# A hybrid attention and MLP layer on one core: modulation in wider pieces loaded ahead, and chunked scores with stacked operands

## The chip, the core and the metric

The kernel runs on one core of one Trainium2 chip. A core has TensorE (PE, matrix multiply, with its weight loads shown as PEld), VectorE (DVE), ScalarE (ACT), GpSimd (POOL) and SyncE (SP), which here issues the DMAs. Every engine works through its own queue in order and waits on semaphores for the others. SBUF is the memory in which tiles lie, 128 partitions wide; PSUM takes the results of matmuls. The metric is the device time of one execution in microseconds; lower is better.

## The reference: what is computed

One layer over a sequence of 1024 tokens of width 1024, all float32. A conditioning vector c gives six modulation vectors; two attention head groups run side by side on one input projection; a gated MLP with a causal convolution follows.

```
mod = silu(c) @ w_ada + b_ada                 # w_ada is 1024 x 6144
sh_a, sc_a, g_a, sh_m, sc_m, g_m = split(mod, 6)

h = rmsnorm(x, g_attn_norm) * (1 + sc_a) + sh_a
q_lat, kv_lat, k_rope, ca_qkv = split(h @ w_in)
# 8 latent heads: up-projections, QK norm over 96, rotary on 32 columns, chunk-causal softmax
# 8 chunked heads: QK norm over 64, each 64-token chunk sees 9 chunks, with a relative bias
s = q @ k.T * scale + bias;  p = softmax(s);  o = p @ v
x = x + g_a * (concat(o_mla, o_ca) @ w_out)

h = rmsnorm(x, g_mlp_norm) * (1 + sc_m) + sh_m
u = causal_conv3(h @ w_up);  x = x + g_m * ((silu(gate) * val) @ w_down)
```

## The kernel before

A float32 product is made of three TensorE products: each operand is split into a rounded high part and the rest, the low part, and hi*hi, hi*lo and lo*hi are summed in PSUM. The split costs an operation on ScalarE (the high part, `hi_of`, line 75) and one on GpSimd or VectorE (the low part, `lo_of`, line 82).

**The start** (lines 194 to 259). The eight 128 x 1024 tiles of x are loaded, their squares summed on ScalarE (212), the root taken on GpSimd (115, 116), and scaled on VectorE (214). The first modulation is `silu(c) @ w_ada` for shift and scale of the mixer. It isn't a matmul: for each of eight blocks `d` of 128 columns the weights (1 MB, `adaw`, two buffers) are multiplied by c and summed on VectorE, 128 x 256 at a time, one tensor-scalar operation and seven fused ones (241, 243), and a matmul with a vector of ones sums over the partitions (246). Then block `d` of x is transposed on TensorE (221), modulated in two halves `h` of 512 tokens on ScalarE, once rounded (224) and once whole (227), and subtracted for the low part on GpSimd (`h` 0) or VectorE (`h` 1) (230): `hT[d, h]`. The first pair of chunked heads is projected as the blocks come (`qk0`, 150 to 152).

After that come the rotary tables (`rope_tables`, 262 to 326, some fifty small VectorE operations on 128 x 128 and two Sin on ScalarE), and the loads of the value weights (`f_v`, `load_w`), whose squares are summed on ScalarE (187) because a power-of-two scale for the values depends on them (`pow2_scale`, 337).

**Attention** is one list of 128 tiles of 128 query rows, first 64 of chunked, then 64 of latent heads. `Unit.scores` (633) does for one tile the score matmuls (655), on VectorE the bias and the row minimum in one operation (670; the scores are negated), on ScalarE the Exp with its row sum (681), the reciprocal (683, 684), on GpSimd the high half of the probabilities in float16 (71, tile `hl`) and on VectorE the low half (703), and then SP issues a DMA transpose of both (714, into `PT`). `Unit.values` (719) comes three tiles later and multiplies with the values (742); each group of four tiles is evicted by ScalarE and VectorE (749, 750). When a pair of heads or a half of the sequence begins, `qk_page` (611) transposes normalised queries and keys on TensorE into PSUM (615) and splits them (618 to 622). In a chunked unit the two heads of a pair lie in partitions 0 to 63 and 64 to 127 of one page, and the matmuls for a head read only its 64.

Between the tiles stand **fillers**, generators that yield after each few projection matmuls: values (`v0`), then the other query and key pairs (`qk1`, ...), the latents (`m`), the two latent up-projections (`up0`, `up1`), and the output projection of the chunked heads (`oca`). `pace` (832) runs them in proportion to the cost of the tiles. While some fillers run, `f_ada` (419) is stepped, the **second modulation**: three more 1024-wide outputs of `silu(c) @ w_ada` in twelve parts of 256 columns. For each it loads eight 128 x 256 tiles (`aw`, 128 KB, line 426) into the three buffers of tag A, which also hold the running sum `aacc` (428, 430). The gate among them is spread over the partitions by a matmul (`gate_bcast`, 451).

The order of instructions on each engine is written by a scheduler that has its own timing of every operation and follows the priorities that the program gives; `issue_after` puts a piece behind a given instruction of its engine's queue in that plan. All DMAs of this text are issued on SP's one queue, in order.

After 656 us come the output projection, the second norm, the MLP and its down projection; the change doesn't touch them.

Of the kernel before, what the change touches and what calls it, by code (L numbers as in the profile page):

```python
# [37 lines left out]
GSTEP, LAG = 2, 4  # L38
DEPTH = 3
OFF_S, OFF_P, OFF_V = 400, 200, 200  # L40
P_BUFS, HL_BUFS, PT_BUFS, TB = 3, 3, 3, 1
# [21 lines left out]
def layer_kernel(ctx, tc, I, out):  # L63
# [76 lines left out]
    def atile(name):  # L140
        return apg.tile([P, 256], F32, name=name, tag="A", bufs=3)

    def pgtile(shape, dt, name):
        return apg.tile(shape, dt, name=name, tag="pg", bufs=6)

    def gemm3(pt, pairs, start=True, stop=True):

        n = len(pairs)
        for i, (sh, sl, mh, ml) in enumerate(pairs):
            pe.matmul(pt, sh, mh, start=(start and i == 0), stop=False)  # L150
            pe.matmul(pt, sh, ml, start=False, stop=False)  # L151
            pe.matmul(pt, sl, mh, start=False, stop=(stop and i == n - 1))  # L152
# [17 lines left out]
    def load_w(name, src, ncol, he="a", ssw=None):  # L170
        tiles = []
        for k in range(ND):
# [7 lines left out]
            for c0 in range(0, ncol, 256):  # L180
# [3 lines left out]
                sp.dma_start(rw, src[:, k, c])  # L184
                if ssw is not None:
# [7 lines left out]

    xs = []
# [6 lines left out]
    wada = []  # L201

    def load_ada(d):
        w = st.tile([P, ND, 2, P], F32, name=f"adaw_{d}", tag="wa", bufs=2)
        sp.dma_start(w[:], I["w_ada_a"][d])
        wada.append(w)

    load_ada(0)
# [8 lines left out]
    def mod_transpose(src, k, h, row, pspool, psum_tag, pb, hpool, tag, tmp, nbuf, veng, leng):  # L217
# [6 lines left out]
        act.activation(pg[:, 0], pt[:], AF.Identity, scale=a, bias=b)  # L224
# [5 lines left out]
        (dve if leng == "v" else pool).tensor_tensor(pg[:, 1], v[:], f32(pg[:, 0]), op=SUB)  # L230
# [4 lines left out]
    qk0 = [ps.tile([P, 1024], F32, name=f"qk0_{i}", tag="S", bufs=2) for i in range(2)]  # L235
    for d in range(ND):
        if d + 1 < ND:
            load_ada(d + 1)
        w = wada[d]
        acc = apg.tile([P, 2, P], F32, name=f"adacc_{d}", tag="A", bufs=3)  # L240
        dve.tensor_scalar(acc[:], w[:, 0], cs[:, 0:1], None, op0=MUL)
        for k in range(1, ND):
            dve.scalar_tensor_tensor(acc[:], w[:, k], cs[:, k:k + 1], acc[:], op0=MUL, op1=ADD)  # L243
        pt = ps.tile([P, 512], F32, name=f"p_ada{d}", tag="mm", bufs=2)
        for i in range(2):
            pe.matmul(pt[:, i:i + 1], acc[:, i, :], ones[:, 0:1], start=True, stop=True)
# [15 lines left out]
    def rope_tables():  # L262
        sp.dma_start(pos_i[:], I["pos"])
        buf = [st.tile([P, 8, NT, 16], F32, name=f"rt{i}", tag="x", bufs=4) for i in range(8)]
        cnt = [0]

        def T():
            cnt[0] += 1
            return buf[(cnt[0] - 1) // 8][:, (cnt[0] - 1) % 8]

        def rnd(src, q):
            o = T()
            dve.tensor_scalar(o, src, q, MAGIC, op0=MUL, op1=ADD)
            dve.tensor_scalar(o, o, MAGIC, None, op0=SUB)
            return o

        def fma(n, c, b):
            o = T()
            dve.scalar_tensor_tensor(o, n, c, b, op0=MUL, op1=ADD)
            return o  # L280

        p1 = _grid(TWO_PI, 2.0 ** -9)
        p2 = _grid(TWO_PI - p1, 2.0 ** -21)
        p3 = TWO_PI - p1 - p2

        def reduce(src):
            n = rnd(src, 1.0 / TWO_PI)
            r = fma(n, -p1, src)
            r = fma(n, -p2, r)
            return fma(n, -p3, r)  # L290

        pf = cst.tile([P, NT], F32, name="pf")
        dve.tensor_copy(pf[:], pos_i[:])
        ang = T()
        dve.tensor_tensor(ang, pf[:].unsqueeze(2).to_broadcast([P, NT, 16]),
                          pk[:, C_INV:C_INV + 16].unsqueeze(1).to_broadcast([P, NT, 16]), op=MUL)
        nh = rnd(ang, 2.0 ** -20)
        rem = fma(nh, -(2.0 ** 20), ang)
        nm = rnd(rem, 2.0 ** -8)
        lo = fma(nm, -(2.0 ** 8), rem)  # L300
        tot = reduce(lo)
        for n, w in ((nh, 2.0 ** 20), (nm, 2.0 ** 8)):
            c = w - round(w / TWO_PI) * TWO_PI
            c1 = _grid(c, 2.0 ** -9)
            x = T()
            dve.tensor_scalar(x, n, c1, None, op0=MUL)
            x = fma(n, c - c1, reduce(x))
            y = T()
            dve.tensor_tensor(y, tot, x, op=ADD)
            tot = y  # L310
        tot = reduce(tot)
        pi_s = 3.1415925
        sn, cn, cl, c2, cl2 = T(), T(), T(), T(), T()
        dve.tensor_scalar(cl, tot, pi_s, -pi_s, op0=MIN, op1=MAX)
        act.activation(sn, cl, AF.Sin)
        dve.tensor_scalar(c2, tot, math.pi / 2, None, op0=ADD)
        dve.tensor_scalar(cl2, reduce(c2), pi_s, -pi_s, op0=MIN, op1=MAX)
        act.activation(cn, cl2, AF.Sin)

        for tab, c0 in ((tabq, C_RQ), (tabk, C_RK)):  # L320
            for half, trig in ((0, cn), (1, sn)):
# [97 lines left out]
    def f_ada():  # L419
        for m in (2, 3, 4):  # L420
            for n in range(4):
                acc = atile(f"aacc{m}_{n}")
                c0 = m * D + n * 256
                for k in range(ND):
# [6 lines left out]
                    if k % 2 and k < ND - 1:  # L431
                        yield 0
# [951 lines left out]
```

## Time and profile before

| | us |
|---|---|
| median of 3 runs | 1423.24 (1422.83 to 1425.13) |
| profiled execution: time | 1430.22 |
| profiled execution: span | 1428.4 |
| busy in the span: TensorE | 1254.2 (88%) |
| VectorE | 1091.0 (76%) |
| ScalarE | 620.7 (43%) |
| GpSimd | 688.8 (48%) |
| first chunked score matmul | 101.0 |
| first latent score matmul | 429.7 |

The profile is one execution. A busy time of a matmul contains its way through the array, so that matmuls in a row overlap; how many ran in a stretch says more than their busy share. A group's row gives line, engine, operation, output and inputs, shapes and the number of instructions, then after the bar the busy time in us and the mean in ns, then the idle time of the engine just ahead of them and what ended it. A row of a stage gives the busy time of each engine with its count, the granted TensorE clock as a share of full speed, the DMA engines' share and GB/s. A row of waits gives engine and line, what it waited for, the sum in us, the number of waits and the longest. The chain of waits is followed back from the last instruction of a stretch, at each step to what released it; shares by engine and line. A row of a DMA gives the size and the median time from issue to landing.

### The profile page before, as it was taken

The numbers are of one execution on the slowest core, as the hardware profiler recorded it, in microseconds if no ns is written. First come the engines' busy times: TensorE is split into PE (matmuls) and PEld (weight loads), VectorE is DVE, ScalarE is ACT, GpSimd is POOL, SyncE is SP. The second block draws the span as 40 slices with busy tenths as digits, with TensorE's granted clock in tenths as the row PEclk, the third lists the DMA queues.
The fourth block names the chain that finished last, engine by engine and source line by source line (L and its number), as shares of the span: only waits on it lengthen the run. The fifth ranks groups of instructions, "written<-read, shape, count | busy, mean of one in ns | idle before, by whom it ended". The sixth has DMA issues, their size and how long they took to land.

```text
span 1428.4 us, 19048 instructions
## 1 busy us (share of the span) xinstructions
PE 1254.2 (88%) x6256; PEld 1027.5 (72%) x6256; DVE 1091.0 (76%) x1891; ACT 620.7 (43%) x1150; POOL 688.8 (48%) x673
## 2 busy tenths in 40 slices
PE   3859989988877688896695999999999999999998
PEld 2749877877756466674573887777778787888886
DVE  6874777855689987794367889889888888688767
ACT  5453344433456544452246442443344434443332
POOL 5263545354545754343572676776768775200000
PEclk9879998999788779896796999999999999999999
DMA  7423656653431667587830333343322223894451
GB/s 285 137 67 82 121 117 141 160 129 89 110 69 39 124 130 169 113 162 198 311 133 10 102 109 133 111 127 124 103 82 98 105 100 103 306 357 132 126 162 59
DMA packets 229743, 190.59 MB, mean 133 GB/s; under 512 B 149382, under 2 KB 180362, under 8 KB 228620
## 3 DMA queue, kind: packets, MB, share of 16 engines
q1 hardware_dynamic: 229644, 189.38, 46.9%
q8 instruction: 49, 0.80, 0.2%
q14 instruction: 50, 0.41, 0.1%
HBM read 117.24 MB, written 37.49 MB: 108 GB/s over the span
## 4 chain that ended last, share of the span: by engine, by line
DVE 34%; PE 28%; DMA 14%; issue 9%; POOL 8%; ACT 6%; SPq 1%; DVEq 0%; POOLq 0%; ACTq 0%
DMA aw<-w_ada 7%; DVE u L1049 5%; DVE u L1048 4%; DMA PTm<-hlm 2%; PE dnA_P L1196 2%; PE dnA_P L1197 2%; PE dnA_P L1198 2%; DVE adacc L243 2%; ACT u L1047 2%; DVE aacc L430 2%; PE dnB_P L1197 1%; PE dnB_P L1198 1%; PE dnB_P L1196 1%; DVE hlm L703 1%; PE sc L655 1%
## 5 line engine op out<-in xcount | busy, mean ns | idle before, releaser
L75 ACT ACTIVATE dnP<-dnr 128x1024 fp32r<-128x1024 f32 x73 | 77.3, 1061 | 110.6 <-PE dnA_P L1198 46.4
L1170 DVE TENSOR_TENSOR dnP<-dnr,dnP 128x1024 fp32r<-128x1024 f32 x72 | 88.3, 1230 | 46.7 <-ACT dnP L75 46.7
L1048 DVE SCALAR_TENSOR_TENSOR u<-c,cvp,u 128x1023 f32<-128x1023 f32 x44 | 82.5, 1915 | 47.1 <-ACT u L1047 47.1
L71 POOL TENSOR_SCALAR hlm<-Pm,rim 128x512 f16<-128x512 f32 (+2 forms) x96 | 68.6, 723 | 88.5 <-DVE rim L684 25.5
L655 PE MATMUL sm<-mk,mq 96*128 96x512 f32 (+3 forms) x288 | 74.4, 388 | 15.8 <-ACT Pm L681 14.9
L1049 DVE SCALAR_TENSOR_TENSOR u<-c,cvp,u 128x1022 f32<-128x1022 f32 x44 | 86.4, 2003 | 0.0
L71 POOL TENSOR_SCALAR hlc<-Pc,ric 128x640 f16<-128x640 f32 (+2 forms) x64 | 44.7, 701 | 83.4 <-DVE ric L684 25.1
L430 DVE SCALAR_TENSOR_TENSOR aacc<-aw,cs,aacc 128x256 f32<-128x256 f32 x84 | 46.6, 555 | 48.1 <-DMA aw<-w_ada 47.6
L681 ACT ACTIVATE Pc<-sc,mc 128x640 f32<-128x640 f32 (+2 forms) x64 | 42.1, 658 | 88.2 <-DVE mc L670 72.4
L703 DVE SCALAR_TENSOR_TENSOR hlm<-Pm,rim,hlm 128x512 f16<-128x512 f32 (+2 forms) x96 | 66.6, 704 | 13.0 <-POOL hlm L71 12.7
L655 PEld LDWEIGHTS sm<-mk,mq 96*128 96x128 f32 x288 | 52.3, 211 | 27.7 <-ACT Pm L681 20.4
L655 PE MATMUL sc<-k,q 64*128 64x512 f32 (+3 forms) x288 | 66.3, 359 | 3.2 <-ACT Pc L681 1.3
L681 ACT ACTIVATE Pm<-sm,mm 128x128 f32<-128x128 f32 (+3 forms) x64 | 47.2, 737 | 44.0 <-DVE mm L674 30.3
L742 PE MATMUL pvm<-PTm,vt 128*128 128x256 f16 (+1 forms) x320 | 47.0, 300 | 16.9 <-DMA PTm<-hlm 13.4
L75 ACT ACTIVATE wc<-ws 128x512 fp32r<-128x512 f32 x22 | 13.9, 633 | 103.8 <-DVE ws L974 97.0
L1047 ACT ACTIVATE u<-c,cvp 128x1024 f32<-128x1024 f32 x44 | 52.1, 1234 | 14.9 <-DVE c L1120 7.9
L655 PEld LDWEIGHTS sc<-k,q 64*128 64x128 f32 x288 | 45.7, 200 | 16.0 <-issue 3.7
L150 PE MATMUL ipq<-wq_s,hT 128*128 128x256 f32 x192 | 56.5, 294 | 0.0
L742 PEld LDWEIGHTS <-vt 128*128 128x128 f16 x320 | 32.7, 111 | 33.0 <-DMA PTm<-hlm 14.8
L703 DVE SCALAR_TENSOR_TENSOR hlc<-Pc,ric,hlc 128x640 f16<-128x640 f32 (+2 forms) x64 | 49.7, 779 | 8.1 <-POOL hlc L71 7.8
L151 PE MATMUL ipq<-wq_s,hT 128*128 128x256 f32 x192 | 55.2, 287 | 0.0
L152 PE MATMUL ipq<-wq_s,hT 128*128 128x256 f32 x192 | 55.1, 287 | 0.0
(404 smaller groups left out, 4477.3 us busy)
## 6 DMA issues: line engine op xcount, KB each, us to landing
wu<-w_up SPq DMA_DIRECT2D x44, 512.0 KB, 3.5
dnr<-g_d SPq DMA_DIRECT2D x73, 256.0 KB, 4.1
aw<-w_ada SPq DMA_DIRECT2D x96, 128.0 KB, 2.3
g_d<-u SPq DMA_DIRECT2D x22, 512.0 KB, 2.8
dnr<-w_down SPq DMA_DIRECT2D x44, 256.0 KB, 5.4
x<-x SPq DMA_DIRECT2D x16, 512.0 KB, 6.5
adaw<-w_ada_a SPq DMA_DIRECT2D x8, 1024.0 KB, 5.1
g_d<-gs SPq DMA_DIRECT2D x22, 256.0 KB, 2.1
```

The lines of the kernel that those rows point to most:

```text
L71: pool.tensor_scalar(o, i, s, 1.0, op0=MUL, op1=MUL)
L75: act.activation(o, i, AF.Copy)
L150: pe.matmul(pt, sh, mh, start=(start and i == 0), stop=False)
L430: dve.scalar_tensor_tensor(acc[:], w[:], cs[:, k:k + 1], acc[:], op0=MUL, op1=ADD)
L655: last = pe.matmul(s[:, c:c + w], qpg[rs_, a, q], kpgs[kh][rs_, b, ko:ko + w], start=(a == 0 and b == 0), stop=(a == 1))
L681: act.activation(pr[:, :n], sv, AF.Exp, bias=m[:], scale=-1.0, accum_out=rsum[:, 0:1])
L703: dve.scalar_tensor_tensor(hl[:, w:2 * w], pp, ri[:], hl[:, :w], op0=MUL, op1=SUB)
L742: last = pe.matmul(dst, u.vst(j), mov, start=(x == 0), stop=(x == len(todo) - 1), skip_group_check=True)
L1047: act.activation(u[:], c, AF.Identity, scale=cvp[:, cv + 2:cv + 3], bias=cvp[:, cv + 3:cv + 4])
L1048: dve.scalar_tensor_tensor(u[:, 1:], c[:, :S - 1], cvp[:, cv + 1:cv + 2], u[:, 1:], op0=MUL, op1=ADD)
L1049: dve.scalar_tensor_tensor(u[:, 2:], c[:, :S - 2], cvp[:, cv:cv + 1], u[:, 2:], op0=MUL, op1=ADD)
L1170: r = f(*a, **k)
```

## The change

- **Start.** The first modulation's weights lie in four pairs of blocks, 512 columns each, loaded in pieces of 512 KB (two of the eight parts of c) into five buffers, the first four pieces ahead of x. Its sums are 128 x 512, and those of the next pair are made while a pair is being transposed. The second halves of a block are copied out of PSUM by VectorE and not by ScalarE.
- The first value weights are loaded and split right after, with rounding and sum of squares on VectorE. Their power-of-two scale is worked out after the first value matmuls. The first pair's normalisation multiply goes from GpSimd to VectorE.
- **Rotary tables** are a generator stepped with each filler step of `qk1`, in two buffers, finished at the latest before the latents.
- **Fillers.** The first 16 filler steps run ahead of the first attention tile, and page transposes are planned behind them. `f_ada` is stepped every 1700 instead of 2000 units of filler cost.
- **Second modulation.** Six parts of 512 columns, 48 loads of 256 KB, each issued three steps ahead of its sum; tag A has five buffers of 512. The loads are planned behind the last transpose, the sums behind the last row minimum.
- **Chunked scores.** For a head the high part of its queries is copied by GpSimd into the other 64 partitions, and the key page holds high and low part of the same head above one another: one matmul over 128 partitions gives hi*hi + hi*lo, and a second over 64 gives lo*hi. Evictions of a page go in halves of 64 partitions.
- **Bias pages** are loaded a unit ahead, in three buffers. The probabilities' tile `hl` has four buffers instead of three, and the scratch for dynamic DMAs is set to 1024.

The core of the diff, with lines left out:

```diff
-P_BUFS, HL_BUFS, PT_BUFS, TB = 3, 3, 3, 1
+P_BUFS, HL_BUFS, TB = 3, 4, 1
 def atile(name):
-    return apg.tile([P, 256], F32, name=name, tag="A", bufs=3)
+    return apg.tile([P, 512], F32, name=name, tag="A", bufs=5)
...
+def load_ada(dd, c):
+    w = st.tile([P, 2, 512], F32, name=f"adaw_{dd}_{c}", tag="wa", bufs=5)
+    sp.dma_start(w[:], I["w_ada_a"][dd][:, 2 * c:2 * c + 2])
+    wada[dd, c] = w
+for c in range(4):
+    load_ada(0, c)
...
+def ada_pair(dd):
+    acc = rtile(f"adacc_{dd}")
+    for k in range(ND):
+        w = wada[dd, k // 2][:, k % 2]
+        if k == 0:
+            dve.tensor_scalar(acc[:], w, cs[:, 0:1], None, op0=MUL)
+        else:
+            dve.scalar_tensor_tensor(acc[:], w, cs[:, k:k + 1], acc[:], op0=MUL, op1=ADD)
+    accs[dd] = acc
+ada_pair(0)
 for d in range(ND):
+    dd, half = divmod(d, 2)
+    if half == 0 and dd + 1 < ND // 2:
+        for c in range(4):
+            load_ada(dd + 1, c)
+        ada_pair(dd + 1)
...
-                 hw, "hT", st, 16, "a", "v" if h else "p")
+                 hw, "hT", st, 16, "v" if h else "a", "v" if h else "p")
...
-rope_tables()
+with tc.issue_after(anchor["lov"]), tc.issue_after(anchor["lop"]):
+    wv0 = load_w("wv0_", I["w_v"][0], 256, he="v", ssw=ssw0,
+                 jt=lambda n: st.tile([P, 512], F32, name=n, tag="hv", bufs=2))
...
 def f_ada():
+    steps = [(m, n, k) for m in (2, 3, 4) for n in range(2) for k in range(ND)]
+    def load(i):
+        if i < len(steps):
+            m, n, k = steps[i]
+            wt[i] = atile(f"aw{m}_{n}_{k}")
+            c0 = m * D + n * 512
+            with tc.issue_after(anchor["sp"]):
+                sp.dma_start(wt[i][:], I["w_ada"][k * P:(k + 1) * P, c0:c0 + 512])
+    for i in range(3):
+        load(i)
...
+        load(i + 3)
+        with tc.issue_after(anchor["dve"]):
...
+                dve.scalar_tensor_tensor(acc[:], wt[i][:], cs[:, k:k + 1], acc[:], op0=MUL, op1=ADD)
...
+def ca_pages(p, g):
+    qn = qns[p, g]
+    half = (slice(0, 64), slice(64, 128))
+    pt = page_psum(lambda j: qn[:, j, 0:128], f"q{p}_{g}", P)
+    qh = [q2(f"qh{p}_{g}_{o}") for o in range(2)]
+    ql = q2(f"ql{p}_{g}")
+    for o in range(2):
+        act.activation(qh[o][half[o]], pt[half[o]], AF.Copy)
+        dve.tensor_tensor(ql[half[o]], pt[half[o]], f32(qh[o][half[o]]), op=SUB)
+        pool.tensor_copy(qh[o][half[1 - o]], f32(qh[o][half[o]]))
+    pt = page_psum(lambda j: qn[:, j, 128:256], f"k{p}_{g}", P)
+    kk = at.tile([P, 2, 512], F32R, name=f"k{p}_{g}", tag="K", bufs=3)
+    for o in range(2):
+        act.activation(kk[half[o], o], pt[half[o]], AF.Copy, scale=gk_ca[half[o]])
+        dve.scalar_tensor_tensor(kk[half[1 - o], o], pt[half[o]], gk_ca[half[o]], f32(kk[half[o], o]),
+                                 op0=MUL, op1=SUB)
+    return (qh, ql), kk
...
+if u.band:
+    qh, ql = qpg
+    for a, rr in ((qh[u.odd], slice(0, P)), (ql, rs_)):
+        for c, ko, w, kh in segs:
+            last = pe.matmul(s[:, c:c + w], a[rr, q], kpgs[kh][rr, u.odd, ko:ko + w],
+                             start=(a is not ql), stop=(a is ql))
...
+    if key == "qk1":
+        if rope[0] is None:
+            rope[0] = rope_tables()
+        with tc.issue_after(anchor["dve"]):
+            next(rope[0], None)
...
-        while nside[0] > 2000:
-            nside[0] -= 2000
+        while nside[0] > 1700:
+            nside[0] -= 1700
...
+with tc.issue_after(anchor["pe"]):
+    for _ in range(NPRE):
+        fill_step()
+first = [anchor["pe"]]
...
-nc = bacc.Bacc("TRN2", target_bir_lowering=False, num_devices=1)
+nc = bacc.Bacc("TRN2", target_bir_lowering=False, num_devices=1, dynamic_dma_scratch_size=1024)
```

More of the change, by code (lines that the diff above doesn't have):

```diff
@@ L151, in gemm3 @@
             pe.matmul(pt, sh, ml, start=False, stop=False)
-            pe.matmul(pt, sl, mh, start=False, stop=(stop and i == n - 1))
+            last = pe.matmul(pt, sl, mh, start=False, stop=(stop and i == n - 1))
+        anchor["pe"] = last.ins
     trail = []
@@ L507, in layer_kernel @@
+    rope = [None]
     G = {}
@@ new lines, in page_psum @@
+    def page_psum(src, name, rows):
+        pt = ps.tile([P, 512], F32, name=f"{name}_ps", tag="T", bufs=TB)
+        with tc.issue_after(first[0]):
+            for j in range(4):
+                pe.transpose(pt[:rows, j * P:(j + 1) * P], src(j), ident[:])
+        return pt
+    def qk_page(src, name, rows, tag, bufs, gain):
+        pt = page_psum(src, name, rows)
+        if gain is None:
+            hi, lo = q2(f"{name}h"), q2(f"{name}l")
+            act.activation(hi[:rows], pt[:rows], AF.Copy)
+            dve.tensor_tensor(lo[:rows], pt[:rows], f32(hi[:rows]), op=SUB)
+            return hi, lo
+        pg = at.tile([P, 2, 512], F32R, name=name, tag=tag, bufs=bufs)
+        act.activation(pg[:rows, 0], pt[:rows], AF.Copy, scale=gain)
+        dve.scalar_tensor_tensor(pg[:rows, 1], pt[:rows], gain, f32(pg[:rows, 0]), op0=MUL, op1=SUB)
+        return pg
```

284 lines of the change are left out of this document (148 added, 136 removed).

## The prediction

> **What bounds the kernel now.** I read the busy times by stage first, cut where the work changes: around the end of the first modulation, to the first score matmul (101.0 us), to 200, to the first score of latent attention (429.6) and to its end.
>
> ```profile
> core 0: us, PE busy (x) PEld busy (x) DVE busy (x) ACT busy (x) POOL busy (x), PEclk, DMA share, GB/s
> 78.20:101.00 22.80, 8.21 (x47) 7.27 (x46) 17.14 (x53) 10.77 (x34) 19.00 (x22) 0.63 0.22 62
> 101.00:200.00 99.00, 97.98 (x725) 87.52 (x725) 62.96 (x183) 40.30 (x95) 45.98 (x57) 1.00 0.46 101
> 200.00:429.60 229.60, 200.76 (x1166) 169.59 (x1165) 159.31 (x470) 100.63 (x278) 111.20 (x177) 0.88 0.52 118
> 429.60:656.50 226.90, 187.52 (x963) 146.18 (x963) 188.62 (x513) 114.69 (x253) 113.99 (x132) 0.86 0.61 123
> ```
>
> Only 101 to 200 is bound by TensorE: 725 matmuls in 99 us, clock 1.00, 0.137 us each. At that pace the 1166 of the next stage need 159 us, VectorE has 159.3 us of work there, and it lasts 229.6: neither is full. The chain of waits of the first 101 us, then of 200 to 429.6, and one row of the waits of that second stretch say why:
>
> ```profile
> by line: DVE adacc L243 24.0%; DMA adaw<-w_ada_a 10.6%; DMA aw<-w_ada 6.3%; DMA x<-x 6.2%; DVE adacc L241 4.5%; POOL ssx L115 3.7%; DVE rt L279 3.5%; DVE hT L230 2.9%; DVE aacc L430 2.8%; POOL rx L116 2.7%; issue 2.4%; DMA wv_r<-w_v 2.3%; P
> by line: DMA aw<-w_ada 34.4%; DVE aacc L430 7.9%; issue 5.9%; DVE hlc L703 4.6%; DMA wq_r<-w_qk 3.5%; PE sc L655 2.8%; DVE m0c L666 2.7%; DMA wqr<-w_qu 2.4%; PE mp L150 2.4%; PE mp L151 2.0%; PE mp L152 2.0%; DVE sc L670 1.8%; SPq L714 1.5%
> DVE aacc L430 <- DMA aw<-w_ada: 39.0, 39, 2.9
> ```
>
> Before 101 us the chain is the first modulation's sums on VectorE: 24.0% and 4.5%, 29 us. From 200 on, 34.4% of it (79 us) is loads of the second modulation and 7.9% (18 us) their sums. Each 128 KB tile is fetched just before its use; VectorE works in order and stands before it 39 times, 39.0 us, with the softmax steps queued behind.
>
> **The change part by part.** Rows for the start:
>
> ```profile
> L243 DVE SCALAR_TENSOR_TENSOR adacc<-adaw,cs,adacc 128x256 f32<-128x256 f32 x56 | 33.7, 605 | 1.1
> L241 DVE TENSOR_SCALAR adacc<-adaw,cs 128x256 f32<-128x256 f32 x8 | 5.3, 658 | 1.5 <-DMA adaw<-w_ada_a 1.5
> L1035 DVE SCALAR_TENSOR_TENSOR gmbc<-adaw,cs,gmbc x14: 737/750/1829, 871.7 to 998.3; 128x512 f32<-128x512 f32 x14
> L1035 DVE SCALAR_TENSOR_TENSOR gmbc<-adaw,cs,gmbc 128x512 f32<-128x512 f32 x14 | 16.1, 1189 | 0.1
> L619 DVE TENSOR_TENSOR q<-q_ps,q 128x512 fp32r<-128x512 f32 x8 | 5.5, 688 | 4.3 <-ACT q L618 4.1
> L230 DVE TENSOR_TENSOR hT<-hv,hT 128x512 fp32r<-128x512 f32 x8 | 6.0, 750 | 0.0
> 17.35 0.75 DVE L214 TENSOR_SCALAR x<-x,rx 128x1024 f32<-128x1024 f32 x1 [0.71 <-POOL rx L116]
> 76.04 0.69 DVE L230 TENSOR_TENSOR hT<-hv,hT 128x512 fp32r<-128x512 f32 x1
> DMA packets 2208, 6.85 MB, mean 342 GB/s; under 512 B 323, under 2 KB 931, under 8 KB 1955
> 84.35 0.69 PE L615 MATMUL q_ps<-ident,qn 128*128 128x128 f32 x2 [6.12 <-POOL qn L373]
> 94.66 0.56 PE L150 MATMUL ipv<-wv_s,hT 128*128 128x256 f32 x1
> 91.37 14.10 SPq L184 DMA_DIRECT2D wq_r<-w_qk  x10
> ```
>
> First modulation in half blocks: 64 sums of 256 columns (39.0 us) become 32 of 512. The same operation at 512 wide is L1035: 0.750 us median, 1.189 mean, where VectorE is slowed. I take 0.85, nearer the median, since GpSimd does little in this stretch: 8 of the 32 run while x still arrives, 24 remain, 20.4 us. Added to VectorE are the 8 second-half copies from PSUM (nearest row L619, 0.688): with the subtractions (0.750) 11.5 us, as before 6.0. Moved ahead are 2 MB of weights: x comes 2.1 MB/342 GB/s = 6.1 us later, so the last x is scaled not at 18.1 us but at 24.2. Then 20.4 + 11.5 + some 2 us of small steps: the last transposed half is ready at 58.1 us, where before it was 76.7: -18.6. The rotary tables, 8 sums of the second modulation and their 6.3% of loads also leave this chain.
>
> What is late next: the weights for the values and for the second pair of heads. In the new order ScalarE's and GpSimd's parts of all 16 tiles stand ahead of the first query page's copies; three are loaded early, three buffers turn over, so 13 loads at 14.10/10 = 1.41 us come after 58.1: 76.4, then landing, split, copies and transposes, some 6 us: first score at 82, against 101.0, **-19**. If the loads start only when the stage has drained, it is 88 to 95; at 0.75 a sum and loads run early, 76. The 16 filler steps put ahead (96 matmuls, where 47 instructions, transposes among them, ran from 78.2 to 101) fill TensorE while it waits; they depend on those weights and on no page.
>
> ```profile
> 62.00:95.00 33.00, 15.82 (x49) 0.60 (x2) 0.68 0.18 53
> 148.39 1.14 PE L655 MATMUL sc<-k,q 64*128 64x256 f32 x6
> 101.00:200.00 99.00, 21.17 (x96) 14.01 (x96) 1.00 0.46 101
> L622 DVE SCALAR_TENSOR_TENSOR k<-k_ps,gk_ca,k 128x512 fp32r<-128x512 f32 x8 | 6.0, 747 | 6.2 <-ACT k L621 6.2
> L71 POOL TENSOR_SCALAR hlc<-Pc,ric 128x512 f16<-128x512 f32 x8 | 6.0, 756 | 14.3 <-DVE ric L684 4.9 <-ACT latT L501 3.4 <-ACT v L410 2.2
> L82 POOL TENSOR_TENSOR wo<-wor,wo 128x512 fp32r<-128x512 f32 x12 | 15.3, 1278 | 12.5 <-ACT wo L75 10.5 <-DVE sm L673 2.0
> L681 ACT ACT_TABLE_LOAD x1 | 1.3, 1283 | 0.0
> ```
>
> 101 to 200. The first row is the rotary tables alone (15.8 us on VectorE), which move here, in among the fillers. The third is the chunked scores in this stage, 96; stacking takes one in three, 32 at 1.14/6 = 0.19 us (second row): 6 us. About 50 value matmuls already done, at 0.137 us: 7 us. TensorE would need 86 us. But VectorE gets 63.0 + 15.8 + 4.5 (three page pairs, each two more operations of 0.69 to 0.75) = 83 us, and as a chain of softmax steps it doesn't run at 96%. I take 95: **-4**, between -13 (TensorE alone) and +3 (VectorE 83% busy, as in latent attention).
>
> The page pairs further cost ScalarE two evictions and GpSimd two copies of 512 columns, no row of this form (between 0.76 of L71 and 1.28 of L82): 16 in all, 12 to 20 us on an engine under half busy; the scores wait for the copies only at a new page. The two Sin evaluations now stand between Exp's, four table loads more at 1.283 us: 5.1 us on ScalarE (40.3 of 99 busy), each pair ahead of one softmax tile, which TensorE's fillers cover; without that cover 5 us. [...]
>
> 200 to 429.6. The second modulation's 96 loads and sums become 48 of double width, loaded three steps ahead.
>
> ```profile
> 101.00:429.60 328.60, 48.86 (x91) 0.92 0.50 113
> L430 DVE SCALAR_TENSOR_TENSOR aacc<-aw,cs,aacc 128x256 f32<-128x256 f32 x77 | 42.2, 548 | 45.8 <-DMA aw<-w_ada 45.3
> aw<-w_ada SPq DMA_DIRECT2D x96, 128.0 KB, 2.3
> DVE bias L761 <- DMA bias<-bias: 1.9, 2, 1.7
> adaw<-w_ada SPq DMA_DIRECT2D x16, 256.0 KB, 3.8
> ```
>
> VectorE's work on them from 101 on is 48.9 us; 48 at 0.85 are 41 (36 to 57 by L1035's two figures), -8, all in the later stage. Twelve more page operations cost 9 there: work 159 + 1 = 160 us. The loads (3.8 us each by the 256 KB row) then have three sums' time ahead; before each stand transposes on SP's queue whose probabilities VectorE wrote, in the new order, some 4 us or more of its own work earlier, by these prices. So the 79 us of loads go from the chain, and what is late next is VectorE itself with its softmax steps, and TensorE at 159 less 64 scores at 0.19 = 147 us. Latent attention, the same steps without such loads, keeps VectorE 188.6/226.9 = 83% busy; 160/0.83 = 193: **-36**. Bounds: VectorE full, -69; the loads still seen, 0.
>
> Bias pages loaded ahead take away at most the 1.9 us of two waits in the row above (95 to 360 us); I count nothing. Fourth probability buffer and the smaller DMA scratch: nothing in latent attention (429.6 to 656.5), where VectorE's instructions are the same; -5 to +5. After 656.5 nothing changes.
>
> Sum: -19 - 4 - 36 = -59 on the profiled execution, whose time is 1430.2 (span 1428.4): 1371. The median of the runs before stands 7.0 lower, 1423.2; so **1364**.
>
> **The rivals.** (1) The loads aren't ahead after all: SP works in order, and a load queued behind a transpose that waits for VectorE is as late as before. For it: SP's queue still mixes both. Against: the distances in the new order. Price: the 36 comes back, 1400. (2) The freed time is used fully: VectorE at 95% from 200 on, 168 us, -61 there, -10 before: 1333. Against: VectorE reaches 83% at best in such a stage. (3) Slower: VectorE takes TensorE's place as the bound and is slowed by GpSimd. If its 512-wide sums cost 1.189 us, work from 200 on is 176 us, and if it stays 69% busy as now (159.3/229.6), the stage lasts 255, +25; with +3 before it and the start at 95 us (-6): 1445. It decides from the point where that share is under 75%, with such sums. For it: L1035's mean is 1.6 times its median. [...] Against: the sums at 256 wide cost 0.605 us at the start, with GpSimd little used, and 0.548 here, beside a busier GpSimd. (4) Only the start moves and the rest cancels: within a few us of 1404.
>
> **How the numbers follow.** The sum's own case, 1333 to 1390: 0.60. Rivals 1 and 4 (1390 to 1412): 0.18. Rival 2 and beyond, under 1333: 0.08. Between 1412 and 1420: 0.02. Within 0.2% (2.8 us, about what a measurement of this kernel can tell from no change): 0.03. Rival 3 and other losses: 0.09. Range 1333 to 1412; faster 0.88, same 0.03, slower 0.09.
>
> **What would show it.** First score matmul at 76 to 90 us; loads of the second modulation under 8% of the chain from there to the first latent score, and VectorE's wait for them under 10 us; that latent score at 350 to 385 us; four more table loads; clock above 0.92 in that stretch; latent attention 220 to 232 us. Wrong if VectorE's wait passes to GpSimd's copies or to SP's queue, or if its 512-wide sums average over 1.1 us.

## The result, and the profile after

The changed kernel takes 1414.07 us (median of 4 runs, 1410.10 to 1414.80) against 1424.16 of the kernel before beside it: ratio 0.9924, interval 0.9903 to 0.9946. So it is faster, by some 11 us and not by 59; 1364 was forecast, and 1414 lies above the range. The profiled execution took 1410.10 (span 1408.3), 20.1 less than the one before, where the medians differ by 10.1: about half of what the two traces differ by is the difference between one execution and another, and a stage's difference of 5 us alone shows nothing.

The stages of the changed kernel by the busy times, cut at its first score, at 200, at its first latent score and just behind the start of the last of them (633.0, where before it was 655.8); they answer to the rows of before.

```profile
core 0: us, PE busy (x) PEld busy (x) DVE busy (x) ACT busy (x) POOL busy (x), PEclk, DMA share, GB/s
101.20:200.00 98.80, 82.63 (x526) 68.17 (x527) 76.20 (x233) 45.39 (x96) 41.62 (x53) 0.86 0.52 118
200.00:424.00 224.00, 195.70 (x1177) 164.02 (x1176) 160.73 (x443) 106.71 (x288) 129.81 (x191) 0.90 0.52 115
424.00:633.50 209.50, 176.93 (x958) 138.39 (x957) 185.63 (x508) 114.05 (x250) 115.96 (x132) 0.91 0.63 133
```

The first score is at 101.2 as before (101.0), the first latent score at 424.0 (429.7). From 101 to 200, where TensorE was full at clock 1.00 with 725 matmuls, it now is busy 82.63 of 98.80 at 0.86 with 526. VectorE's share from 200 on is 160.73/224 = 72%, before 69%, and not 83%.

The first latent score thus comes 5.7 us earlier. More of what the two traces differ by lies behind it, from there to the last eviction of latent attention: 241.0 us before, 227.0 after, where nothing was forecast. What follows then takes the same time to within 1 us. The kernel before and the changed one:

```profile
429.60:670.60 241.00, 194.41 (x1003) 151.06 (x1002) 195.32 (x524) 118.48 (x259) 116.92 (x136) 0.85 0.62 126
```

```profile
424.00:651.00 227.00, 182.64 (x995) 142.51 (x993) 192.83 (x521) 118.97 (x258) 120.61 (x138) 0.89 0.65 138
```

The chain of waits from 200 to 424, and VectorE's waits for the second modulation's loads from 101.2 to 424 (sum, times, longest):

```profile
by line: issue 7.8%; DVE hlc L794 6.7%; PE sc L740 5.7%; PE pvc L833 5.4%; DMA aw<-w_ada 5.3%; PE mp L153 3.9%; DMA PTc<-hlc 3.8%; PE mp L154 3.7%; PE mp L155 3.6%; DVE m0c L757 3.5%; DMA wm_r<-w_m 2.7%; DVE sc L761 2.7%; DVE aacc L404 2.5%
DVE aacc L404 <- DMA aw<-w_ada: 5.5, 5, 1.5
DVE aacc L402 <- DMA aw<-w_ada: 1.0, 1, 1.0
```

The loads did go: from 34.4% of this chain to 5.3%, the waits from 39 us to 6.5. Nothing took their place as one item; probabilities, scores, values, latents and transposes share it. Both stages from the first chunked to the first latent score in one row each, the kernel before and then the changed one:

```profile
101.00:429.60 328.60, 298.75 (x1889) 257.11 (x1889) 222.27 (x652) 140.93 (x373) 157.18 (x233) 0.92 0.50 113
```

```profile
101.20:424.00 322.80, 278.33 (x1701) 232.19 (x1701) 236.93 (x673) 152.09 (x383) 171.44 (x243) 0.89 0.52 116
```

TensorE has 188 matmuls less here. By these rows its busy time falls 20.4 us, of which the lower clock has already taken back some. In the stretches at clock 0.50 (54.6 us of the stage before, 71.7 after) TensorE was busy 47.3 us before and 55.2 after; half of that, 24 and 28 us, is an estimate of what the clock cost: in the changed kernel's trace 128x512 float32 matmuls in a row start 0.427 us apart at 0.50 and 0.227 at 1.00 (medians). At full clock the work fell by some 24 us, 0.13 us for each of the 188 matmuls; of those 4 went to the clock, 15 to more idle time (29.9 to 44.5), and 6 are left. That is the account of the stage: work was taken from an engine that then waited.

### The profile page after: what moved, and what is told of

Its sections match the earlier page's. It is cut to its first block, busy times and chain, and to the rows that moved or that the text cites. A ratio compares the mean times of both kernels' runs of the same rounds, so it can differ in the third digit from the quotient of the medians.

```text
span 1408.3 us, 18699 instructions
## 1 busy us (share of the span) xinstructions
PE 1234.5 (88%) x6156; PEld 1006.3 (71%) x6156; DVE 1093.0 (78%) x1861; ACT 624.0 (44%) x1132; POOL 709.3 (50%) x685
## 3 DMA queue, kind: packets, MB, share of 16 engines
q1 hardware_dynamic: 223592, 189.38, 47.3%
## 4 chain that ended last, share of the span: by engine, by line
DVE 35%; PE 30%; issue 10%; DMA 9%; POOL 8%; ACT 7%; SPq 1%; POOLq 0%; DVEq 0%; ACTq 0%
DVE u L1157 5%; DVE u L1156 4%; PE dnA_P L1304 2%; PE dnA_P L1305 2%; PE dnA_P L1306 2%; ACT u L1155 2%; DVE hlc L794 2%; PE dnB_P L1306 1%; PE dnB_P L1305 1%; PE dnB_P L1304 1%; DVE hlm L794 1%; DMA wor<-w_out 1%; DMA aw<-w_ada 1%; PE sc L740 1%; PE sm L746 1%
## 5 line engine op out<-in xcount | busy, mean ns | idle before, releaser
L794 DVE SCALAR_TENSOR_TENSOR hlc<-Pc,ric,hlc 128x640 f16<-128x640 f32 (+2 forms) x64 | 53.0, 830 | 10.0 <-POOL hlc L72 9.3
L833 PE MATMUL pvm<-PTm,vt 128*128 128x256 f16 (+1 forms) x320 | 43.2, 284 | 12.6 <-DMA PTm<-hlm 8.8
L1232 ACT ACTIVATE u<-u 128x1024 f32<-128x1024 f32 x22 | 23.3, 1061 | 67.9 <-DVE u L1157 67.9
L83 POOL TENSOR_TENSOR wc<-ws,wc 128x512 fp32r<-128x512 f32 x22 | 34.3, 1558 | 36.4 <-ACT wc L76 36.4
L1306 PE MATMUL dnA_P<-dnP 128*128 128x512 f32 x132 | 51.4, 389 | 0.0
L1305 PE MATMUL dnA_P<-dnP 128*128 128x512 f32 x132 | 51.4, 389 | 0.0
L1304 PE MATMUL dnA_P<-dnP 128*128 128x512 f32 x132 | 51.2, 389 | 0.0
L83 POOL TENSOR_TENSOR wd<-wu,wd 128x512 fp32r<-128x512 f32 x22 | 30.4, 1382 | 37.5 <-ACT wd L76 37.5
```

The source lines that it names most:

```text
L83: (pool if eng == "p" else dve).tensor_tensor(o, i, f32(hi), op=SUB)
L794: dve.scalar_tensor_tensor(hl[:, w:2 * w], pp, ri[:], hl[:, :w], op0=MUL, op1=SUB)
L1304: pe.matmul(pt, sh, w[:, 0, 0], start=start, stop=False, skip_group_check=add)
L1305: pe.matmul(pt, sh, w[:, 1, 0], start=False, stop=False, skip_group_check=add)
L1306: pe.matmul(pt, sl, w[:, 0, 0], start=False, stop=stop, skip_group_check=add)
```

## The experiments

Ratios are against the kernel before, measured beside each run (1423.5 to 1426.9); the changed kernel's is 0.9924. "Stage" is from the first chunked to the first latent score.

| run | median us | ratio, interval |
|---|---|---|
| changed kernel | 1414.1 | 0.9924, 0.9903 to 0.9946 |
| ada: before + second modulation | 1413.8 | 0.9931, 0.9912 to 0.9950 |
| adaold: changed - second modulation | 1422.3 | 0.9985, 0.9966 to 1.0004 |
| noaw: before, 84 loads left out | 1406.5 | 0.9881, 0.9852 to 0.9910 |
| hl4: before + fourth hl | 1427.8 | 1.0031, 1.0015 to 1.0048 |
| hl3: changed - fourth hl | 1419.9 | 0.9973, 0.9954 to 0.9992 |
| npre0: changed - fillers ahead | 1417.3 | 0.9932, 0.9908 to 0.9956 |
| score1: changed - stacked scores | 1414.7 | 0.9927, 0.9902 to 0.9952 |
| rope0: changed, tables at the start | 1423.6 | 0.9987, 0.9966 to 1.0008 |
| start0: changed - first modulation | 1418.2 | 0.9949, 0.9926 to 0.9971 |
| noada: changed, sums left out | 1398.4 | 0.9817, 0.9803 to 0.9832 |
| cut: changed, a third of fillers' products out | 1395.2 | 0.9795, 0.9771 to 0.9820 |
| d4: changed, values four tiles behind | 1417.0 | 0.9959, 0.9938 to 0.9980 |
| r15, r13, r11: changed, ratio 1.5, 1.3, 1.1 | 1405.5, 1403.4, 1419.2 | 0.9845, 0.9859, 0.9972 |
| b_r13: before, ratio 1.3 | 1433.0 | 1.0056, 1.0029 to 1.0083 |
| ada_r13: ada, ratio 1.3 | 1419.7 | 0.9967, 0.9947 to 0.9986 |
| score1_r13: score1, ratio 1.3 | 1401.5 | 0.9812, 0.9790 to 0.9835 |

**What the loads were worth (noaw).** In the kernel before:

```diff
-                    w = atile(f"aw{m}_{n}_{k}")
-                    sp.dma_start(w[:], I["w_ada"][k * P:(k + 1) * P, c0:c0 + 256])
+                    if k == 0:
+                        w = atile(f"aw{m}_{n}_{k}")
+                        sp.dma_start(w[:], I["w_ada"][k * P:(k + 1) * P, c0:c0 + 256])
```

> The kernel before with 84 of the 96 loads of the second modulation left out: each part loads its first tile only and adds it eight times (the modulation is then another one; all sums stay). Theory L (the prediction's: the loads' 79 us of the chain from 200 on are worth some 36): 1380 to 1395. Theory S (behind the loads stand the softmax steps, which set the pace of chunked attention anyway): 1410 to 1424, with VectorE's wait for aw gone and chunked attention as long as before within 8 us.

1406.5, 17 us faster: neither theory's number, and nearer to S. In its trace some 7.6 came at the start (first score 93.4: eight of the second modulation's sums stood ahead of it, and their loads were 6.3% of that chain, 6.4 us) and some 11 in the stage (317.4 instead of 328.6). noaw's busy times by stage, then its chain of waits from 200 to its first latent score:

```profile
101.00:200.00 99.00, 97.88 (x742) 88.94 (x741) 63.99 (x179) 39.54 (x92) 48.29 (x57) 1.00 0.40 83
200.00:410.80 210.80, 195.03 (x1157) 165.61 (x1156) 155.07 (x462) 100.23 (x277) 111.35 (x175) 0.90 0.43 90
...
by line: PE sc L656 13.9%; DMA PTc<-hlc 10.8%; PE pvc L743 8.5%; PE mp L150 4.8%; PE ipv L150 4.5%; PE ipv L152 4.3%; PE ipv L151 4.3%; PE mp L152 4.1%; PE mp L151 4.0%; PE ipq L152 3.9%; PE ipq L150 3.7%; PE ipq L151 3.6%; issue 3.4%; DVE 
```

With no loads to wait for, the chain passes to TensorE: scores, values, latents and projections are its items, and TensorE is busy 195.0 of 210.8 us. VectorE's share is 74%. So 79 us of the chain were worth 17 us at the end.

**The second modulation alone (ada), and all but it (adaold).** ada takes the changed `f_ada`, the five wide buffers and the planned places of loads and sums into the kernel before, stepped every 2000:

```diff
-        return apg.tile([P, 256], F32, name=name, tag="A", bufs=3)
+        return apg.tile([P, 512], F32, name=name, tag="A", bufs=5)
-                    sp.dma_start(w[:], I["w_ada"][k * P:(k + 1) * P, c0:c0 + 256])
+            load(i + 3)
```

adaold is the changed kernel with the old `f_ada` and three buffers of 256.

> The kernel before with the second modulation of the changed kernel alone (512 wide, three steps ahead, five buffers, smaller scratch; step every 2000). Theory L: 1385 to 1395, and then another part of the change cost what this gained. Theory S: 1412 to 1426.

> The changed kernel with the second modulation as before (256 wide, loaded just before use, three buffers). Theory L (its loads ahead are the whole gain): 1422 to 1430. Theory R (the rest of the change gains as much by itself, and the two overlap): 1412 to 1418.

ada gives 1413.8, all of the whole change's gain (Theory S); adaold gives 1422.3, its interval holding no change (in time Theory L). So the rest of the change is worth next to nothing as it stands. ada's scores, first and last start after the duration in ns:

```profile
L671 PE MATMUL sc<-k,q x288: 215/336/789, 89.5 to 386.0; 64*128 64x128 f32 x48, 64*128 64x384 f32 x41, 64*128 64x512 f32 x28, 64*128 64x256 f32 x27
```

Its first score is at 89.5, 11.5 us earlier than before, although its first modulation is the old one; its stage, 89.5 to 424.1, is 334.6 and no shorter. The part that was forecast to shorten the stage by 36 moved the start, and the stage not at all; latent attention is 8 us shorter than before in that trace.

**The start (npre0, start0, rope0).**

```diff
-NPRE = 16
+NPRE = 0
```

```diff
-    ada_pair(0)
     for d in range(ND):
-        dd, half = divmod(d, 2)
...
+        if d + 1 < ND:
+            load_ada(d + 1)
+        w = wada[d]
+        acc = rtile(f"adacc_{d}")[:, :256].rearrange("p (a b) -> p a b", a=2)
```

```diff
+    rope[0] = rope_tables()
+    for _ in rope[0]:
+        pass
     with tc.issue_after(anchor["pe"]):
         for _ in range(NPRE):
```

> The changed kernel without the 16 filler steps ahead of the first attention tile. Theory F (TensorE's order: those steps hold the first score behind value and query weights, so the 10.7 us that the first modulation gained never reach the tiles): first score at 80 to 92 instead of 101.2, time 1402 to 1410. Theory S (softmax steps set the pace, the fillers have to run anyway and stand idle time out elsewhere): first score earlier too, time 1411 to 1420.

> The changed kernel with the first modulation as before (eight blocks of 256 columns, 1 MB loads behind x, ScalarE's second copies); value weights, rotary tables, fillers ahead and the rest as changed. Theory A (the first modulation's gain reaches the end): transposed halves ready at 73 to 78 and first score 8 to 12 us later than 101.2, time 1420 to 1428. Theory B (it is lost again among the chunked tiles): 1411 to 1418.

> The changed kernel with the rotary tables whole ahead of the first filler step instead of in between the steps of the second pair's filler. Theory V (VectorE's 15.8 us among the first softmax steps cost the stage as much as they saved at the start): 1408 to 1416, first score 5 to 14 us later, tiles 4 to 20 that much closer together. Theory 0 (they were free among the tiles): 1420 to 1430.

Without the filler steps ahead (npre0) the first score is at 91.1 and the first latent score at 417.9, 6 us earlier than in the changed kernel, and the time is the same: Theory S. With the old first modulation (start0) the last transposed half is ready at 69.9 and not at 73 to 78, against 66.7; the first score is hardly later (101.7), and the time is about 4 us more with overlapping intervals: nearer B, not settled. With the rotary tables at the start (rope0) the first score is at 106.1 and the time 9 us more: Theory 0, the tables were nearly free among the tiles. What held the first score at 101.2 shows in the changed kernel's TensorE groups and waits from 66 to 101.2, and in its busy times while the filler steps run:

```profile
L154 PE MATMUL ipv<-wv_s,hT 128*128 128x256 f32 x44 | 14.5, 330 | 4.4 <-POOL wv_s L83 4.2
...
PE ipv L154 <- POOL wv_s L83: 4.2, 3, 3.5
```

```profile
73.00:86.60 13.60, 8.67 (x33) 7.50 (x34) 7.15 (x27) 1.25 (x3) 12.19 (x15) 0.50 0.27 78
86.60:93.00 6.40, 6.40 (x55) 6.40 (x54) 0.08 (x1) 2.45 (x6) 3.80 (x6) 1.00 0.34 105
```

The value matmuls wait for GpSimd's part of the weights (3.5 us at once), which stands behind the normalisation's roots there; TensorE falls to half clock for 13.6 us, and the score pages stand behind the last of those matmuls in TensorE's order. The query weights of the second pair were late as well: their loads, issued from 78.4 us on, are 28.6% of the chain of these 35 us, its largest item.

**Stacked scores (score1).** `prep` calls `qk_page` again for queries and keys, and the band branch of `scores` is off:

```diff
-                pages["c", p, g] = ca_pages(p, g)
+                q = qk_page(lambda j: qns[p, g][:, j, 0:128], f"q{p}_{g}", P, "Q", 2, None)
+                k = qk_page(lambda j: qns[p, g][:, j, 128:256], f"k{p}_{g}", P, "K", 3, gk_ca[:])
+                pages["c", p, g] = (q, k)
```

> The changed kernel with the chunked scores as before (three matmuls over 64 partitions, pages evicted whole, no GpSimd copies). Theory P (TensorE's work sets the stage, as the prediction's sum had it): 96 matmuls of some 0.19 us come back, 18 us: 1426 to 1434. Theory S (TensorE idles 100 us between first chunked and first latent score, so its matmuls are free there): 1409 to 1418, idle time down by 10 us or more.

1414.7, the same time: Theory S. With 93 matmuls more in the stage TensorE is idle less (320.2 - 288.6 = 31.6 us instead of 44.5), at a better clock (0.91 against 0.89), and the stage is 320.2 long instead of 322.8:

```profile
100.30:420.50 320.20, 288.57 (x1794) 245.87 (x1794) 226.81 (x663) 143.33 (x367) 159.78 (x229) 0.91 0.52 116
```

**The fourth probability buffer (hl4, hl3).** hl4 is the kernel before with the fourth buffer and the change's smaller scratch; hl3 takes it from the changed kernel.

```diff
-P_BUFS, HL_BUFS, PT_BUFS, TB = 3, 3, 3, 1
+P_BUFS, HL_BUFS, PT_BUFS, TB = 3, 4, 3, 1
```

> The kernel before with a fourth buffer for the probabilities' tile hl (and the smaller DMA scratch that makes room for it), nothing else. Theory N (the prediction's own step: nothing in latent attention): 1419 to 1427. Theory H (in latent attention the wait of transposed probabilities, 15.1% of its chain before and 3.9% after, is a wait for a free hl buffer): latent attention 10 to 20 us shorter, 1404 to 1414.

> The changed kernel with three hl buffers instead of four. Theory N: 1410 to 1418. Theory H: 1424 to 1434, with the wait for transposed probabilities back at 10% or more of the chain of latent attention.

Both theories fall, Theory N by only 0.8 and 1.9 us. In the kernel before the buffer costs 4 us; in the changed one it brings some 7 by the ratios. In hl3 transposed probabilities are 10.9% of the chain of latent attention again, as Theory H had it, and yet the time stays below its range. TensorE's wait for transposed probabilities from 424 to 656, in the changed kernel and in hl3:

```profile
PE pvm L833 <- DMA PTm<-hlm: 8.8, 6, 5.4
```

```profile
PE pvm L833 <- DMA PTm<-hlm: 27.5, 17, 4.8
```

In the kernel before and hl4 the same wait is 10.6 and 16.9: with the buffer it grew there. From the first latent score to the last eviction the changed kernel needs 227.0 us, hl3 237.2, the kernel before 241.0, hl4 243.0, ada (three buffers) 232.7, start0 (four) 244.9. ada_r13 (three) needs 246.7. The length doesn't follow the buffers, and the changed kernel's is the shortest of all. What sets it between 227 and 247 wasn't found; with one trace of each kernel, it isn't shown either how much of it changes from one execution to the next.

**What bounds the changed kernel (noada, cut, d4).** noada leaves out 42 of 48 loads and sums, cut leaves hi*lo out of the products of six fillers, and d4 lets the values follow four tiles behind.

```diff
+                if k:
+                    return
...
-                else:
-                    dve.scalar_tensor_tensor(acc[:], wt[i][:], cs[:, k:k + 1], acc[:], op0=MUL, op1=ADD)
```

```diff
-            pe.matmul(pt, sh, ml, start=False, stop=False)
+            if not two:
+                pe.matmul(pt, sh, ml, start=False, stop=False)
```

```diff
-DEPTH = 3
+DEPTH = 4
```

> The changed kernel with 42 of the 48 loads and sums of the second modulation left out (each part is its first product only). Theory V (VectorE, at 83% of a stage, is what is left as the bound, as the prediction's sum for 200 to 430 had it): some 36 us of VectorE go, 1370 to 1385. Theory M (VectorE and TensorE take turns: stretches full of fillers wait for TensorE, stretches of tiles for the softmax steps in series): 1398 to 1410. Theory P (TensorE alone): 1411 to 1417.

> The changed kernel with hi*lo left out of the products of the fillers v0, qk1 to qk3, v1 and the latents (384 of 1152 matmuls, 46 us or more of TensorE between first filler and first latent score; the order paced as before). Theory P: 1362 to 1378. Theory M: less than half of it, 1392 to 1406. Theory V: 1410 to 1417.

> The changed kernel with the values four tiles behind their scores instead of three. Theory Q (the serial steps of one tile, over the number of tiles in flight, set the pace of the tiles): 1390 to 1406. Theory M or V: within 5 us of 1414, either way.

noada: 1398.4, cut: 1395.2, d4: 1417.0. Taking 27 us from VectorE's stage (236.9 to 209.9, in the row below) shortened it by 22 and the end by 16. In cut the stage has 340 matmuls less (1701 to 1361) and 38 us less busy time; it is 28 us shorter, and the end came 19 earlier. In both, latent attention took 10 and 12 us longer than in the changed kernel. noada leaves out loads too, so that 6.5 us of waits went with its sums; the share of either wasn't measured. More tiles in flight brought nothing. The rows of noada and of cut:

```profile
101.20:401.90 300.70, 273.25 (x1701) 231.71 (x1702) 209.87 (x631) 149.62 (x381) 163.99 (x243) 0.91 0.42 88
```

```profile
96.50:391.40 294.90, 240.51 (x1361) 193.54 (x1362) 234.77 (x673) 151.55 (x383) 172.49 (x243) 0.86 0.57 127
```

So Theory M holds as to sizes: either engine's work counts, neither in full. In cut the clock falls further, to 0.86: fewer matmuls, and more busy time at half speed (70.6 us instead of 55.2).

**Fillers among the tiles (r13, r11, r15, b_r13, ada_r13, score1_r13).** One number is changed, the fillers' cost per cost of a chunked tile:

```diff
-R_CA, R_MLA = 1.9, 0.5
+R_CA, R_MLA = 1.3, 0.5
```

> The changed kernel with fewer fillers among the chunked tiles (ratio 1.3 instead of 1.9 of the tiles' cost), so that more of them run in a stretch by themselves where a unit needs them. Theory M: 1422 to 1440, TensorE's idle time from first chunked to first latent score up by 8 us or more. Theory V: within 4 us of 1414.

> The kernel before with the ratio of fillers to chunked tiles at 1.3 instead of 1.9. Theory C (the pacing counts the stacked scores at their old three matmuls, and only that made 1.9 too much): within 4 us of 1424 or slower. Theory G (at 1.9 the fillers among the tiles stand in TensorE's order ahead of ready scores in either kernel): 1410 to 1418.

> The kernel before with the new second modulation and ratio 1.3. Theory C: 1410 to 1418, as with 1.9. Theory G: 1400 to 1407, as the whole change with 1.3 (1403.4), and then start, stacked scores and rotary tables are worth next to nothing.

> The changed kernel with the ratio at 1.1. If fillers among the tiles only delay, 1396 to 1402. If 1.3 is near the balance (fewer leave them to run by themselves while VectorE idles), 1402 to 1412.

> The changed kernel with the chunked scores as before and ratio 1.3. Theory C (the cheaper scores, counted at their old cost, make 1.9 too much): 1413 to 1424, no faster than with 1.9 (1414.7). Theory D (the rest of the change, the filler steps run ahead among it, moved the balance): 1400 to 1408.

> The changed kernel with ratio 1.5. Theory C or D: between 1403 and 1412, on the way from 1.3 to 1.9. Theory E (each ratio gives another order of instructions, and orders differ by some 8 us with no rule): anywhere from 1402 to 1424, above 1414 above all.

r13 turned Theory M's forecast round: 1403.4, faster by some 10 us, with less idle time and not more. Then Theory C had b_r13 right (slower, 1.0056) and ada_r13 nearly (0.9967, 1.7 above its range), but score1_r13 ends it: with scores as before the same ratio gives 1401.5, faster still. Theory D's range holds it, and r15 lies at 1405.5, within the noise of 1.3 and well off 1.9; r11, at 1419.2, is outside both of its forecasts, and at 1.1 the gain is gone. So 1.9 does better than 1.3 in the kernel before and worse in the changed one, and the stacked scores aren't why; by the ratios they even cost some 7 us at 1.3. Theory E, that each ratio only gives another order and no rule holds, isn't excluded: all four ratios lie within its range. Which of the other parts moved it (fillers run ahead, the first modulation, the tables) stays open; the second modulation alone didn't, since ada gets slower with 1.3. The stage of r13 and of score1_r13:

```profile
100.30:410.50 310.20, 272.95 (x1713) 229.26 (x1714) 236.54 (x673) 152.79 (x383) 168.92 (x243) 0.93 0.54 121
```

```profile
98.80:413.20 314.40, 283.25 (x1809) 240.95 (x1810) 223.86 (x659) 144.65 (x368) 161.41 (x229) 0.95 0.52 119
```

The same work as in the changed kernel, but in r13 TensorE is busy 37.7 us at half clock instead of 55.2, which by the estimate above costs 19 us instead of 28, and is idle 37.3 instead of 44.5. score1_r13, the changed kernel less its stacked scores with ratio 1.3, is the fastest here that does all of the work: 0.9812 against 0.9924.

## Why the prediction was wrong

**200 to 429.6, -36: this step failed.** That the loads would leave the chain was right (under 8%: 5.3; waits under 10 us: 6.5). Wrong was that VectorE would be late next, "keeps VectorE 188.6/226.9 = 83% busy; 160/0.83 = 193". The 83% was carried over from latent attention, with 963 matmuls in 226.9 us, to a stage with 1166 in 229.6. There the share stayed at 72% in the changed kernel and at 74% with the loads gone (noaw), where TensorE is the fuller engine, busy 195.0 of 210.8. What the runs show in its place is a stage that neither engine sets alone: from the first chunked to the first latent score, 27 us less of VectorE's work shortened it by 22 (noada), and a fifth of TensorE's matmuls less by 28 (cut). The loads themselves were worth 17 us of time in the kernel before, with 7.6 of them in the start. And TensorE's 147 us were counted at the pace of clock 1.00, while this stage ran at 0.88 before and 0.90 after.

VectorE's work from 200 on, forecast as 160 and measured as 160.7, agrees by luck. The sums were put there with 41 us; 25.8 are there and 12.4 stand before 200. The twelve further page operations, 9 us, were eight (16 instead of 8 of 0.7 us), and the low halves of the chunked probabilities (line 794) took 37.1 us instead of 33.1, which no run explains. Both stages together were forecast at 243 and measured at 236.9.

**The start, -19: this step failed too.** The transposed halves were forecast for 58.1 and are ready at 66.7. VectorE's groups from the last x on, 25.9 to 66.7:

```profile
L256 DVE SCALAR_TENSOR_TENSOR adacc<-adaw,cs,adacc 128x512 f32<-128x512 f32 x21 | 19.3, 926 | 0.3
L238 DVE TENSOR_SCALAR hv<-ht_ps,modT 128x512 f32<-128x512 f32 x8 | 6.4, 802 | 4.4 <-ACT hT L233 4.4
L239 DVE TENSOR_TENSOR hT<-hv,hT 128x512 fp32r<-128x512 f32 x8 | 6.4, 801 | 0.1
L254 DVE TENSOR_SCALAR adacc<-adaw,cs 128x512 f32<-128x512 f32 x3 | 3.4, 1135 | 0.0
```

x was scaled 1.7 us later than 24.2; the 24 sums took 22.7 instead of 20.4; copies and subtractions 12.8 instead of 11.5; and 4.4 us of waits for ScalarE at the last blocks weren't in the sum. That is the size. As to the price of a sum: with no GpSimd instruction beside it a sum at L256 took 0.733 to 0.752 us (18 of 28), beside one 0.750 to 1.797 (10), and GpSimd, counted as doing little here, was busy 18.1 of these 40.8 us. The step after it failed in kind: that the filler steps "fill TensorE while it waits" took them for free. They need the very weights that were late, so they ran behind them and ahead of the first score, partly at half clock: 101.2, where npre0 has 91.1. Without them the first score comes 22.8 us behind the last half (68.3 in npre0), near the 24 of the sum; with them 34.5. But npre0 takes the same time as the changed kernel, so the earlier first score was worth nothing there, which the sum didn't allow for. The gain of the second modulation's leaving the start, 11.5 us in ada, was not seen as its own.

**101 to 200, -4, and the stacked scores:** of no value here, since TensorE stopped being the bound of that stretch (82.6 of 98.8 busy, clock 0.86). That TensorE's 86 us of the sum come near these 82.6 is luck: 526 matmuls ran where the sum left 643. VectorE's terms there were about right in sum: 83 forecast, 76.2 measured. The upper bound was worked out wrongly: 83 us at 83% are 100, +1 and not +3. The rotary tables were nearly free among the tiles (rope0), and the four further table loads came; two of them:

```profile
166.42 1.28 ACT L549 ACT_TABLE_LOAD   x1
167.72 0.31 ACT L549 ACTIVATE rt<-rt 128x128 f32<-128x128 f32 x1
168.04 1.28 ACT L772 ACT_TABLE_LOAD   x1
```

The Sin starts when its table is in, 1.30 us after the load began; what ran before had ended at the load's start (166.40).

**Latent attention, 0 within 5:** this step failed too, to the good: from the first to the last score it went from 226.9 to 209.5 us in the profile, 14 us to the last eviction, more than the 5.7 us of all stages ahead of it. The instructions were nearly the same, as foreseen (995 matmuls, before 1003); over the runs the same stage took 227 to 247 us. So in these two traces the larger part of the gain doesn't lie where the sum had put it, and it has no known cause.

**Bias pages, 0:** loaded a unit ahead, they were to take away at most 1.9 us of waits. VectorE's waits for them between the first chunked and the first latent score are 5.4 us in the changed kernel. No run tests what that costs.

**The rivals.** (2) is out by the same 72%. (1) is out: the loads were ahead. (3), slower by VectorE, stood on two conditions: its share did stay under 75%, but its 512-wide sums cost 0.808 and not 1.189 us:

```profile
L404 DVE SCALAR_TENSOR_TENSOR aacc<-aw,cs,aacc 128x512 f32<-128x512 f32 x42 | 33.9, 808 | 5.8 <-DMA aw<-w_ada 5.5
```

Sums did run longer beside GpSimd: in the kernel before, the six of L1035 with no GpSimd instruction beside them took 0.737 to 0.741 us, the eight beside one 0.748 to 1.829, six of them over 1.7. At L404 the 14 with none took 0.671 to 0.752, the 28 beside one 0.730 to 1.298, with a median of 0.751: the slowing was there, and small on the whole.

(4), the start moves and the rest cancels, came nearest in time and was wrong in place: what moves the start by itself is the second modulation (ada), and in the changed kernel the filler steps ahead cancel that. Of the signs that were named, the first score at 76 to 90 us, the clock above 0.92, the first latent score at 350 to 385 us and latent attention at 220 to 232 us failed, at 101.2, 0.90, 424 and 209.5.

## What to carry to other kernels

A wait's share of the chain isn't its price: leave the awaited work out once, and see what the chain names next; here 79 us were worth 17. Where two engines with like loads are woven together by a fixed ratio, work taken from one of them can return as idle time, and another ratio is worth trying (1.9 to 1.3: 1414 to 1403 us); a busy share of another stage says nothing about it. Filler that needs what the first tile waits for doesn't fill that wait, though here leaving it out brought no time either.

## What the hardware showed beyond that

In the traces before and after, the clock that TensorE was granted is 1.00 or 0.50, and each of the 45 stretches at one clock that end within the execution, in either trace, lasted a multiple of 3.413 us (3.41 to 484.7). In the changed kernel it fell to half behind slices of that length in which TensorE was only partly idle. Slices of it, each with the one behind it:

```profile
148.10:151.50 3.40, 1.66 (x12) 1.00 (x9) 3.31 (x10) 2.17 (x4) 2.73 (x3) 0.99 0.01 2
151.50:154.90 3.40, 1.08 (x4) 0.71 (x4) 3.29 (x13) 1.40 (x3) 0.29 (x1) 0.50 0.71 138
168.50:171.90 3.40, 1.62 (x12) 1.28 (x13) 1.83 (x11) 3.39 (x8) 1.08 (x2) 1.00 0.46 102
171.90:175.30 3.40, 3.40 (x16) 2.68 (x13) 2.93 (x8) 1.57 (x6) 3.40 (x4) 0.51 0.57 136
219.70:223.10 3.40, 1.81 (x16) 1.30 (x14) 3.31 (x6) 1.29 (x5) 1.47 (x3) 1.00 0.86 150
223.10:226.50 3.40, 0.27 (x1) 0.27 (x2) 3.29 (x8) 1.64 (x6) 2.34 (x2) 0.51 0.80 187
```

Behind slices with 1.66, 1.62 and 1.81 of 3.40 us busy the next ran at 0.50 to 0.51. In the changed kernel's whole trace all 23 falls follow a slice with 21 to 58% busy (though one slice of 51% was followed by none), and the full clock came back only behind a slice with 85% or more; in the kernel before, falls stand behind slices of up to 75%, and in cut one return stands behind 81%. So these are bounds of what was seen and not thresholds. Idle time of 1.6 us in one slice (3.40 less 1.81) thus stood ahead of a slice at half clock, and in the changed kernel each of the nine slices at half clock that were 65 to 82% busy was followed by another at half.
